# A hybrid decoder layer: one more shared pair, a combination that writes PSUM from VectorE, and other first and last transfers

## The chip, the core and the metric

The kernel runs on one core of a Trainium2 chip. The metric is the device time of one execution in microseconds (us). PE is TensorE (matmuls), DVE is VectorE, ACT is ScalarE, POOL is GpSimd, and SP is the engine that issues most transfers. PSUM is the memory that matmuls add up in; DVE and ACT can read and write it too.

## The reference

One decoder layer on 256 rows of width 2048, in float32. `SPLITS` cuts the projection into the gated recurrence's part (convolution, recurrent scan, gelu gate) and retention's part (rotary q and k, decayed scores, group norm, swish gate). The feed-forward width is 5632.

```
u = rmsnorm(h, ln1_w[l])
proj = jnp.einsum('bsd,de->bse', u, w_in[l])
lru_x, lru_g, q, k, v, ret_g = jnp.split(proj, SPLITS, axis=-1)
...
y = jnp.concatenate([y_lru, y_ret], axis=-1)
h = h + jnp.einsum('bse,ed->bsd', y, w_out[l])
u = rmsnorm(h, ln2_w[l])
ff = jax.nn.silu(jnp.einsum('bsd,df->bsf', u, w_ffn_gate[l])) * jnp.einsum('bsd,df->bsf', u, w_ffn_up[l])
h = h + jnp.einsum('bsf,fd->bsd', ff, w_ffn_down[l])
...
return rmsnorm(h, final_norm_w)
```

## The kernel before

**Split products.** Each operand is split in two float32r parts: ACT casts (`wh`, L122) and DVE subtracts (`wl`, L123). A product of two such operands is three matmuls, `wh` x `ah`, `wl` x `ah` and `wh` x `al`, in `three` (L682 to L684). One matmul has 128 stationary columns and 512 moving ones.

**Pairs.** From the out-projection on, a product is done by pairs of 128-row slices of the contraction: a 2 x 2 arrangement of left parts (a11 ... a22, the two halves of the 256 rows) and of weight parts (b11 ... b22, 512 columns each), into four PSUM accumulators c11, c12, c21, c22. A *plain* pair (letter `p` in `STEPS`, or two letters `h` for its halves) takes 8 products, 24 matmuls. A *shared* pair takes 7: its sums (t1 to t4 from the weights, L660; s1 to s4 from the left parts) go in four products that are made during the block before (`s`, function `share`, 12 matmuls) and three that are made in the pair's own block (`d`, `direct`, 9 matmuls, for which the second weight half is loaded and split again). For a shared pair DVE forms t1 to t4 in place (`add`). `SUMMED` lists the shared pairs of each block.

**Combination.** After the last `s` of a block, the four accumulators of `share` hold sums that are still to be combined: c11 stays, and c12, c22 and c21 are computed from all four (L806 to L812) and written back to PSUM, where the next block's own products are added on top. There are 13 such combinations, blocks 1 to 12 and the first of the two down blocks.

**Blocks and order.** Blocks 0 and 1 are the out-projection, 2 to 12 the gate/up projection (512 columns of w_gu each), then two blocks of the down projection. After a gate/up block, ACT's Silu and a DVE step (L878) give `gated`, which PE turns (`ft`, L867) into the left operand of the down projection. `make_left(i)` casts and splits such a left operand; the down block calls it before the weights of pair i. `program` is the list of steps; each step's loads are issued `AHEAD` = 3 ahead of it on SP's queue, and the Tile framework orders each engine's instructions by its own estimate of times. `hooks` names what is done at a given pair of the down blocks: `rows_back` brings residual rows back from DRAM by POOL's queue, and `load_fw` loads the final norm's weights there. Weights pass through 7 raw buffers and the pools of `split_tiles`; 60 buffers of 512 columns (`act_tile`) hold most of the rest.

**Start.** The first product is `v`: for each k of 16, x's slice of 128 columns is scaled to `u` (L297, L298) by ACT and DVE, from `small` (norm weights and biases, 104 columns), and PE runs 6 matmuls (L173 to L175). `load_x` issues the slices between the weight halves: `small`, slices 0 and 1 apart, then pairs. `squares` later sums the squares of x by ACT and POOL.

## Time and profile before

| | us |
|---|---|
| median of 3 runs | 1082.88 (1081.78 to 1082.94) |
| the profiled execution | 1082.31 |
| its span, first to last instruction | 1080.5 |
| PE busy | 1069.9 (99%) |
| DVE busy | 965.8 (89%) |
| ACT busy | 664.4 (61%) |
| POOL busy | 55.8 (5%) |
| mean granted TensorE clock | 0.998 |

The span leaves out 1.8 us around the program. "Busy" counts an engine's instructions; PE's matmuls overlap, so a row's duration is longer than the distance to the next one. A row such as `PE c L682 <- ACT sh L122: 0.3, 1, 0.3` says that PE, at line 682, waited for ACT's result of line 122: in all, how often, and the longest.

### The profile page before, as it was taken

The numbers are of one execution on the slowest core, as the hardware profiler recorded it, in microseconds if no ns is written. First come the engines' busy times: TensorE is split into PE (matmuls) and PEld (weight loads), VectorE is DVE, ScalarE is ACT, GpSimd is POOL, SyncE is SP. The second block draws the span as 40 slices with busy tenths as digits, with TensorE's granted clock in tenths as the row PEclk, the third lists the DMA queues.
The fourth block names the chain that finished last, engine by engine and source line by source line (L and its number), as shares of the span: only waits on it lengthen the run. The fifth ranks groups of instructions, "written<-read, shape, count | busy, mean of one in ns | idle before, by whom it ended". The sixth has DMA issues, their size and how long they took to land.

```text
span 1080.5 us, 14585 instructions
## 1 busy us (share of the span) xinstructions
PE 1069.9 (99%) x5086; PEld 896.5 (83%) x5086; DVE 965.8 (89%) x1400; ACT 664.4 (61%) x948; POOL 55.8 (5%) x73
## 2 busy tenths in 40 slices
PE   9999999999999999999999999999999999999997
PEld 7888888888888888888888888888888888888886
DVE  7789899988878889989999999999989899997994
ACT  7656744468746776656656565665656666555562
POOL 0602230000000000000000000000000000001001
PEclk9999999999999999999999999999999999999999
DMA  9964575554557588667777777787776846567562
GB/s 330 349 213 155 176 252 164 188 176 156 195 195 234 180 306 278 233 228 252 258 273 227 258 255 239 259 279 234 252 256 210 291 141 213 184 203 277 189 220 78
DMA packets 71387, 244.62 MB, mean 226 GB/s; under 512 B 8209, under 2 KB 8593, under 8 KB 71313
## 3 DMA queue, kind: packets, MB, share of 16 engines
q1 hardware_dynamic: 68400, 236.34, 64.2%
q0 software_dynamic: 1472, 4.72, 1.3%
q10 hardware_dynamic: 1440, 2.62, 0.6%
q8 instruction: 40, 0.66, 0.2%
q14 instruction: 35, 0.28, 0.1%
HBM read 239.46 MB, written 4.19 MB: 225 GB/s over the span
## 4 chain that ended last, share of the span: by engine, by line
PE 96%; POOL 1%; DVE 1%; DMA 1%; issue 0%; ACT 0%; SPq 0%; POOLq 0%; ACTq 0%
PE c L684 22%; PE c L683 22%; PE c L682 22%; PE fm L193 10%; PE fm L195 5%; PE tm L173 3%; PE tm L174 3%; PE tm L175 3%; POOL sumsq L309 1%; PE p L683 1%; PE p L682 1%; PE p L684 1%; PE ft L867 1%; DMA x<-in_x 1%; PE ht L587 0%
## 5 line engine op out<-in xcount | busy, mean ns | idle before, releaser
L122 ACT CAST wh<-raw 128x1024 fp32r<-128x1024 f32 (+1 forms) x499 | 463.0, 960 | 323.7 <-PE c L684 124.5
L123 DVE TENSOR_TENSOR wl<-raw,wh 128x1024 fp32r<-128x1024 f32 (+1 forms) x499 | 542.1, 1114 | 71.4 <-ACT wh L122 69.4
L683 PE MATMUL c<-wl,ah 128*128 128x512 f32 x820 | 320.0, 390 | 0.0
L684 PE MATMUL c<-wh,al 128*128 128x512 f32 x820 | 317.1, 389 | 0.0
L682 PE MATMUL c<-wh,ah 128*128 128x512 f32 x820 | 285.5, 391 | 0.0
L682 PEld LDWEIGHTS c<-wh,ah 128*128 128x128 f32 x820 | 153.9, 188 | 31.9 <-ACT wh L122 0.3
L684 PEld LDWEIGHTS c<-wh,al 128*128 128x128 f32 x820 | 153.9, 188 | 31.9 <-DVE al L123 0.3
L683 PEld LDWEIGHTS c<-wl,ah 128*128 128x128 f32 x820 | 154.0, 188 | 31.5
L193 PE MATMUL fm<-u,wh 128*128 128x512 f32 x512 | 161.3, 396 | 0.0
L195 PEld LDWEIGHTS fm<-u,wl 128*128 128x128 f32 x512 | 96.0, 188 | 22.5
L195 PE MATMUL fm<-u,wl 128*128 128x256 f32 x512 | 100.9, 278 | 0.0
L660 DVE TENSOR_TENSOR raw<-raw,raw 128x512 f32<-128x512 f32 x116 | 79.7, 687 | 2.2 <-DMA raw<-in_w_down 0.4
L660 DVE TENSOR_TENSOR raw<-raw 128x512 f32<-128x512 f32 x116 | 78.9, 685 | 1.1
L193 PEld LDWEIGHTS fm<-u,wh 128*128 128x128 f32 x512 | 78.3, 189 | 0.3
L683 PE MATMUL c<-wl,sh 128*128 128x512 f32 x193 | 74.8, 389 | 0.0
L684 PE MATMUL c<-wh,sl 128*128 128x512 f32 x193 | 73.6, 389 | 0.0
L682 PE MATMUL c<-wh,sh 128*128 128x512 f32 x193 | 68.3, 391 | 0.3 <-ACT sh L122 0.3
L174 PE MATMUL tm<-wl,u 128*128 128x512 f32 x128 | 48.6, 392 | 0.0
L175 PE MATMUL tm<-wh,u 128*128 128x512 f32 x128 | 48.5, 390 | 0.0
L173 PE MATMUL tm<-wh,u 128*128 128x512 f32 x128 | 46.6, 393 | 1.4 <-ACT u L297 1.4
L1118 POOL DMA_DIRECT2D htok<-kept_rows x8 | 4.3, 542 | 794.9 <-DVE wl L123 704.1
L682 PEld LDWEIGHTS c<-wh,sh 128*128 128x128 f32 x193 | 36.2, 188 | 8.2 <-ACT sh L122 0.7
(249 smaller groups left out, 1062.0 us busy)
## 6 DMA issues: line engine op xcount, KB each, us to landing
raw<-in_w_gu SPq DMA_DIRECT2D x216, 512.0 KB, 5.1
raw<-in_w_down SPq DMA_DIRECT2D x91, 512.0 KB, 4.6
raw<-in_w_out SPq DMA_DIRECT2D x34, 512.0 KB, 3.8
raw<-in_w_lx SPq DMA_DIRECT2D x16, 512.0 KB, 6.7
raw<-in_w_k SPq DMA_DIRECT2D x16, 512.0 KB, 3.7
raw<-in_w_q SPq DMA_DIRECT2D x16, 512.0 KB, 3.8
raw<-in_w_rg SPq DMA_DIRECT2D x16, 512.0 KB, 3.5
raw<-in_w_lg SPq DMA_DIRECT2D x16, 512.0 KB, 3.5
```

The costliest lines, as they stand in the source:

```text
L122: act.copy(out=dst_h, in_=src)
L123: v.tensor_tensor(out=dst_l, in0=src, in1=dst_h.bitcast(F32), op=ALU.subtract)
L173: pe.matmul(ps, ah, wh, start=first, stop=False)
L174: pe.matmul(ps, ah, wl, start=False, stop=False)
L175: pe.matmul(ps, al, wh, start=False, stop=last)
L193: pe.matmul(ps, wh, hl, start=n + i == 0, stop=False)
L195: pe.matmul(ps[:, :S], wl, hl[:, :S], start=False, stop=n + i == len(order) - 1)
L309: pool.tensor_tensor(out=sumsq, in0=sumsq, in1=sq, op=ALU.add)
L660: v.tensor_tensor(out=dst, in0=a, in1=b, op=ALU.add)
L682: pe.matmul(p, ah, bh, start=first, stop=False, skip_group_check=onto)
L683: pe.matmul(p, ah, bl, start=False, stop=False, skip_group_check=onto)
L684: pe.matmul(p, al, bh, start=False, stop=last, skip_group_check=onto)
```

## The change

1. The last gate/up block shares four pairs where it shared three: pair 0 is no longer plain. `STEPS` of block 11 becomes that of blocks 4 to 10, and block 12 takes block 11's old one. PE's program goes from 5027 to 5024 rows.
2. In the combination, c21 is also copied to SBUF (`p7`), c12 is written by DVE's subtraction straight to PSUM, c22 is rewritten in place by a `scalar_tensor_tensor`, and c21 is ACT's copy of q.
3. `make_left(1)` to `make_left(4)` become steps of their own inside block 12.
4. The first slice of x and `small` come as one transfer `lead` (128 x 360); slices 1 and 2, 3 and 4, ... come in pairs, slice 15 alone. One buffer of rows is taken from the act pool instead, so its load comes elsewhere on SP's queue.
5. In the second down block the final norm's weights are loaded at pair 9 instead of 11, and the rows come back at pair 12 instead of 7.

```diff
-SUMMED = ((), (4, 5), (2, 3), (1, 2, 3)) + ((0, 1, 2, 3),) * 8 + ((1, 2, 3),)
+SUMMED = ((), (4, 5), (2, 3), (1, 2, 3)) + ((0, 1, 2, 3),) * 9
...
-STEPS = ("pppspppspp", "ppspdpsdpp", "pdpsdpspspp", "pspsdpsdpsdp") + ("psdhsdhsdhsdhp",) * 7 + ("psdpsdpsddp", "psdpsdpsdpp")
+STEPS = ("pppspppspp", "ppspdpsdpp", "pdpsdpspspp", "pspsdpsdpsdp") + ("psdhsdhsdhsdhp",) * 8 + ("psdpsdpsddp",)
...
+ASIDE = {(12, 0): 1, (12, 2): 2, (12, 4): 3, (12, 6): 4}
...
-    xpool = early.enter_context(tc.tile_pool(name="resid", bufs=8))
+    xpool = early.enter_context(tc.tile_pool(name="resid", bufs=7))
+    lpool = early.enter_context(tc.tile_pool(name="lead", bufs=1))
...
+    lead = lpool.tile([P, S + N_SMALL], F32, tag="lead", name="lead")
+    last = lpool.tile([P, S], F32, tag="last", name="last")
+    small = lead[:, S:]
...
-        return xt[k // 2][:, (k % 2) * S : (k % 2) * S + S]
+        if k in (0, KT - 1):
+            return last if k else lead[:, :S]
+        return xt[(k - 1) // 2][:, (k - 1) % 2 * S : (k - 1) % 2 * S + S]
...
-        htok[cb, t] = res_tile("htok")
+        htok[cb, t] = (res_tile if n else act_tile)("htok")
...
-            p1, p, q = (act_tile(x) for x in ("p1", "p", "q"))
+            p1, p7, p, q = (act_tile(x) for x in ("p1", "p7", "p", "q"))
             act.copy(out=p1, in_=ps["c11"])
+            act.copy(out=p7, in_=ps["c21"])
             v.tensor_tensor(out=p, in0=ps["c12"], in1=p1, op=ALU.subtract)
-            v.tensor_tensor(out=q, in0=p, in1=ps["c22"], op=ALU.subtract)
-            act.copy(out=ps["c12"], in_=q)
-            v.tensor_tensor(out=ps["c22"], in0=q, in1=ps["c21"], op=ALU.subtract)
-            v.tensor_tensor(out=ps["c21"], in0=ps["c21"], in1=p, op=ALU.subtract)
+            v.tensor_tensor(out=ps["c12"], in0=p, in1=ps["c22"], op=ALU.subtract)
+            v.tensor_tensor(out=q, in0=p7, in1=p, op=ALU.subtract)
+            v.scalar_tensor_tensor(
+                out=ps["c22"], in0=ps["c22"], scalar=-1.0, in1=q, op0=ALU.mult, op1=ALU.subtract
+            )
+            act.copy(out=ps["c21"], in_=q)
...
+                if (self.index, k) in ASIDE:
+                    program.append(([], lambda i=ASIDE[self.index, k]: make_left(i)))
                 program.append(([quad], run))
...
         if k == 0:
-            nc.sync.dma_start(out=small, in_=A["small"])
-        if k < 2:
-            nc.sync.dma_start(out=xt[0][:, k * S : k * S + S], in_=A["x"][0][:, k * S : k * S + S])
-        elif k % 2 == 0:
+            nc.sync.dma_start(out=lead, in_=A["lead"])
+        elif k == KT - 1:
+            nc.sync.dma_start(out=last, in_=A["last"])
+        elif k % 2:
             nc.sync.dma_start(out=xt[k // 2], in_=A["x"][k // 2])
...
-        rows_back(1, act_tile)
-
-    hooks = {0: {6: stop_more, 9: swap_back}, 1: {7: sums_end, 11: load_fw}}
+
+    hooks = {0: {6: stop_more, 9: swap_back}, 1: {7: sums_end, 9: load_fw, 12: lambda: rows_back(1, act_tile)}}
```

The first rows of SP's queue, before (names are buffers; `raw` are weights, halves of 128 x 512):

```order
L140 DMA raw_4_125<-in_w_v 128x512
L1028 DMA small_90<-in_small 128x104
L1030 DMA x_0_82<-in_x 128x256
L140 DMA raw_4_125<-in_w_v 128x512
L1030 DMA x_0_82<-in_x 128x256
L140 DMA raw_9_143<-in_w_v 128x512
L1032 DMA x_1_83<-in_x 128x512
L140 DMA raw_9_143<-in_w_v 128x512
L140 DMA raw_14_159<-in_w_v 128x512
L1032 DMA x_2_84<-in_x 128x512
L140 DMA raw_14_159<-in_w_v 128x512
```

and after:

```order
L146 DMA raw_4_128<-in_w_v 128x512
L1043 DMA lead_85<-in_lead 128x360
L146 DMA raw_4_128<-in_w_v 128x512
L1047 DMA x_0_87<-in_x 128x512
L146 DMA raw_9_145<-in_w_v 128x512 x2
L1047 DMA x_1_88<-in_x 128x512
L146 DMA raw_14_161<-in_w_v 128x512 x2
L1047 DMA x_2_89<-in_x 128x512
L146 DMA raw_19_177<-in_w_v 128x512 x2
L1047 DMA x_3_90<-in_x 128x512
```

`small` and one transfer of x are gone, `lead` is wider, and x's pairs begin with slice 1, one place earlier than the pair of slices 2 and 3 stood.

DVE around the last combination, in block 12, before (c12_1668, c22_1666 and c21_1667 are the down block's accumulators; wl are splits of weights):

```order
L123 TENSOR_TENSOR wl_1729_8192<-raw_1727_8189,wh_1728_8191 128x1024
L123 TENSOR_TENSOR wl_1721_8152<-raw_1719_8149,wh_1720_8151 128x1024
L123 TENSOR_TENSOR wl_1726_8162<-raw_1722_8155,wh_1725_8161 128x1024
L808 TENSOR_TENSOR p_1714_8126<-c12_1668_7925,p1_1713_8125 128x512
L809 TENSOR_TENSOR q_1715_8127<-p_1714_8126,c22_1666_7917 128x512
L123 TENSOR_TENSOR wl_1734_8202<-raw_1730_8195,wh_1733_8201 128x1024
L811 TENSOR_TENSOR c22_1666_7917<-q_1715_8127,c21_1667_7921 128x512
L812 TENSOR_TENSOR c21_1667_7921<-c21_1667_7921,p_1714_8126 128x512
```

and after (c12_1693, c22_1691; L893 is the old L878, on block 12's own accumulators):

```order
L129 TENSOR_TENSOR wl_1749_8239<-raw_1747_8236,wh_1748_8238 128x1024
L129 TENSOR_TENSOR wl_1752_8245<-raw_1750_8242,wh_1751_8244 128x1024
L129 TENSOR_TENSOR wl_1746_8224<-raw_1744_8221,wh_1745_8223 128x1024
L819 TENSOR_TENSOR p_1739_8197<-c12_1693_8000,p1_1737_8195 128x512
L129 TENSOR_TENSOR wl_1760_8287<-raw_1758_8284,wh_1759_8286 128x1024
L129 TENSOR_TENSOR wl_1757_8281<-raw_1755_8278,wh_1756_8280 128x1024
L820 TENSOR_TENSOR c12_1693_8000<-p_1739_8197,c22_1691_7992 128x512
L821 TENSOR_TENSOR q_1740_8198<-p7_1738_8196,p_1739_8197 128x512
L129 TENSOR_TENSOR wl_1772_8344<-raw_1765_8328,wh_1771_8343 128x1024
L893 SCALAR_TENSOR_TENSOR gated_1753_8254<-c12_1601_7599,r2_tok_113,gated_1753_8254 128x512
L893 SCALAR_TENSOR_TENSOR gated_1754_8262<-c22_1599_7591,r2_tok_113,gated_1754_8262 128x512
L822 SCALAR_TENSOR_TENSOR c22_1691_7992<-c22_1691_7992,q_1740_8198 128x512
```

p and the writes of the accumulators now stand further apart; two splits stand between p and c12, and block 12's last two gated steps ahead of c22. The order of the three results was c12 (through q and ACT), c22, c21 and is c12, q for c21, c22.

PE at the end of block 12, before (c_1587 to c_1590 belong to block 12, c_1665 to c_1668 to the down block):

```order
L683 MATMUL c22_1588_7565<-wl_1721_8152,ah_847_4128 128x512
L684 MATMUL c22_1588_7565<-wh_1720_8151,al_848_4129 128x512
L682 MATMUL c11_1665_7913<-wh_1725_8161,ah_1723_8157 128x512
L683 MATMUL c11_1665_7913<-wl_1726_8162,ah_1723_8157 128x512
L682 MATMUL c12_1668_7925<-wh_1725_8161,ah_1723_8157 128x512
L683 MATMUL c12_1668_7925<-wl_1726_8162,ah_1723_8157 128x512
L682 MATMUL c22_1666_7917<-wh_1725_8161,ah_1723_8157 128x512
L683 MATMUL c22_1666_7917<-wl_1726_8162,ah_1723_8157 128x512
L682 MATMUL c21_1667_7921<-wh_1725_8161,ah_1723_8157 128x512
```

and after, where c12 begins (c_1690 is c11; its first row stands directly behind block 12's last, 15 matmuls ahead of c12's):

```order
L692 MATMUL c11_1690_7988<-wh_1756_8280,ah_1721_8121 128x512
L693 MATMUL c11_1690_7988<-wl_1757_8281,ah_1721_8121 128x512
L694 MATMUL c11_1690_7988<-wh_1756_8280,al_1722_8122 128x512
L692 MATMUL c11_1690_7988<-wh_1759_8286,ah_1658_7856 128x512
L693 MATMUL c11_1690_7988<-wl_1760_8287,ah_1658_7856 128x512
L694 MATMUL c11_1690_7988<-wh_1759_8286,al_1659_7857 128x512
L692 MATMUL c12_1693_8000<-wh_1745_8223,ah_1710_8078 128x512
L693 MATMUL c12_1693_8000<-wl_1746_8224,ah_1710_8078 128x512
```

Before, the four accumulators of the down block are all used within its first 7 matmuls; after, five pairs' products onto c11 come first, then those onto c12, c21 and c22.

More of the change, by code (lines that the diff above doesn't have):

```diff
@@ L93, in aux @@
         return paux.tile([P, 512], F32, tag="aux", name=nm(name))
+    lead = lpool.tile([P, S + N_SMALL], F32, tag="lead", name="lead")
+    last = lpool.tile([P, S], F32, tag="last", name="last")
+    small = lead[:, S:]
     xt = []
-    for i in range(KT // 2):
+    for i in range(KT // 2 - 1):
         xt.append(xpool.tile([P, 512], F32, tag="xh", name=f"x_{i}"))
-    small = cpool.tile([P, N_SMALL], F32, name="small")
     def xs(k):
-        return xt[k // 2][:, (k % 2) * S : (k % 2) * S + S]
+        if k in (0, KT - 1):
+            return last if k else lead[:, :S]
+        return xt[(k - 1) // 2][:, (k - 1) % 2 * S : (k - 1) % 2 * S + S]
     ident = cpool.tile([P, P], F32, name="ident")
@@ L306, in squares @@
             sq = act_tile("sq") if i else sumsq
-            act.activation(out=sq, in_=xt[i], func=AF.Square)
+            if i < KT // 2 - 1:
+                act.activation(out=sq, in_=xt[i], func=AF.Square)
+            else:
+                act.activation(out=sq[:, :S], in_=lead[:, :S], func=AF.Square)
+                act.activation(out=sq[:, S:], in_=last, func=AF.Square)
             if i:
@@ L1216, in cols @@
         return a.reshape(-1, P).T
+    x = g["x"][0].T.reshape(KT, P, S)
     arrays = {
-        "x": g["x"][0].T.reshape(KT // 2, 2, P, S).transpose(0, 2, 1, 3).reshape(KT // 2, P, 512),
-        "small": np.concatenate(
+        "x": x[1:-1].reshape(KT // 2 - 1, 2, P, S).transpose(0, 2, 1, 3).reshape(KT // 2 - 1, P, 512),
+        "last": x[-1],
+        "lead": np.concatenate(
             [
+                x[0],
                 cols(g["ln1_w"][0]), cols(g["ln2_w"][0]), cols(g["conv_w"][0].reshape(-1)), cols(g["conv_b"][0]),
```

## The prediction

> **What bounds the kernel now.** I read the first part of the page, then the waits of TensorE (PE), then windows over the stages that the change touches, then the timeline of the first 12 us.
>
> ```profile
> PE 1069.9 (99%) x5086; PEld 896.5 (83%) x5086; DVE 965.8 (89%) x1400; ACT 664.4 (61%) x948; POOL 55.8 (5%) x73
> ```
>
> Each entry is an engine's busy time and its share of the span. PE is never free for long; DVE is the next one. The waits of PE (who waited, for whom, us in total, times, the longest) name what it waited for by this profile; a row on the warm-up is left out:
>
> ```profile
> PE tm L173 <- ACT u L297: 1.4, 2, 0.9
> ...
> PE c L682 <- ACT sh L122: 0.3, 1, 0.3
> ```
>
> So a gain can come from fewer matmuls, or from the 1.4 us at the start. A loss comes from any engine that lets PE wait. Windows over two early full gate/up blocks, and then over the last two (from one block's transposes to the next's), show how near DVE is to that; columns are PE, PEld, DVE, ACT, POOL busy, the granted clock, DMA share and rate:
>
> ```profile
> 526.01:568.84 42.83, 42.83 (x195) 35.54 (x194) 40.72 (x52) 25.69 (x34) 0.00 (x0) 1.00 0.76 262
> 568.84:610.78 41.94, 41.94 (x191) 34.78 (x190) 39.98 (x52) 25.64 (x34) 0.00 (x0) 1.00 0.76 245
> ...
> 776.33:820.79 44.46, 44.46 (x202) 36.82 (x201) 40.05 (x53) 25.36 (x34) 0.00 (x0) 1.00 0.72 244
> 820.79:861.36 40.57, 40.57 (x184) 33.40 (x183) 37.07 (x51) 27.30 (x35) 0.00 (x0) 1.00 0.76 259
> ```
>
> In 526.01 to 610.78 DVE is busy 80.70 of 84.77 us (95%) and PE has no gap. In the last two blocks DVE has 77.12 of 85.03 us, so 7.9 us free.
>
> **Part 1: three matmuls fewer.** A plain pair costs 24 matmuls; a shared one costs 12 in the block before it and 9 in its own. PE has 5024 rows after, 5027 before. The spacing is read from PE's timeline at the end of block 12, of which these are the first and the last of 14 rows:
>
> ```profile
> 849.66 0.39 PE L683 MATMUL c<-wl,ah 128*128 128x512 f32 x1
> ...
> 852.61 0.39 PE L683 MATMUL c<-wl,ah 128*128 128x512 f32 x1
> ```
>
> (852.61 − 849.66)/13 = 0.227 us each (the 0.39 overlap). Three fewer give −0.68 us, all of it on the path, since PE has no gap there.
>
> The price is on DVE. The newly shared pair needs four sums (L660), three splits of 512 columns and two of 1024 where plain needs two of 1024. The rows give the shortest, median and longest in ns:
>
> ```profile
> L660 DVE TENSOR_TENSOR raw<-raw,raw x116: 678/686/695, 303.0 to 1037.9; 128x512 f32<-128x512 f32 x116
> ...
> L123 DVE TENSOR_TENSOR wl<-raw,wh x499: 673/1217/2318, 4.2 to 1049.6; 128x1024 fp32r<-128x1024 f32 x131, 128x512 fp32r<-128x512 f32 x36
> L123 DVE TENSOR_TENSOR t4l<-raw,t4h x45: 678/683/687, 306.8 to 841.6; 128x512 fp32r<-128x512 f32 x45
> ...
> L122 ACT CAST wh<-raw x499: 603/1051/1118, 3.5 to 1045.6; 128x1024 fp32r<-128x1024 f32 x131, 128x512 fp32r<-128x512 f32 x36
> L122 ACT CAST t4h<-raw x45: 611/617/626, 305.3 to 838.5; 128x512 fp32r<-128x512 f32 x45
> ```
>
> The split of the 1024-wide forms takes 1.22 us (the median; most of the 499 are that wide), the 512-wide 0.68. In block 11, which does the share: four sums 4 × 0.686 = 2.74, the splits of b11, t2 and t4 3 × 0.68 = 2.05, that of t1 and t3 together 1.22: +6.0 us. In block 12 the second half alone is loaded and split, 1.22 in place of 2.44: −1.2 us. So DVE gets 4.8 us more in a stretch with 7.9 us free, which leaves about 3.1 less the 0.68 that PE gives up, 2.4 of 84.4 us, or 97% busy. The row nearest to that is one block that ran at this share and cost PE nothing:
>
> ```profile
> 484.95:526.01 41.06, 41.06 (x188) 34.03 (x186) 39.72 (x52) 25.98 (x35) 0.00 (x0) 1.00 0.75 259
> ```
>
> 39.72 of 41.06 is 97%, over half the length. I take 0 for the wait of PE and keep as its other end that none of the free time can be used: 4.8 us of DVE work plus PE's own 0.68, or 5.5. ACT casts the same columns, block 11's more by 3 × 0.62 + 1.05 = 2.9 us; that and the 512 KB which block 12 reloads are costed at nothing: ACT is busy 25 to 27 us of a 41 to 44 us window, and the DMA share there is 0.72 to 0.76. Without that cover the 2.9 us would be PE's.
>
> **Part 2: the combination, 13 times.** Before: two copies on ACT, four operations on DVE. After: three copies, still four on DVE.
>
> ```profile
> L807 ACT COPY p<-c x13: 569/575/589, 328.6 to 839.0; 128x512 f32<-128x512 f32 x13
> ...
> L809 DVE TENSOR_TENSOR q<-p,c x13: 676/678/686, 332.1 to 848.1; 128x512 f32<-128x512 f32 x13
> ...
>   ACT c L810: 7.4, 5
> ...
> L811 DVE TENSOR_TENSOR c<-q,c x13: 684/686/689, 333.9 to 849.8; 128x512 f32<-128x512 f32 x13
> ...
> L878 DVE SCALAR_TENSOR_TENSOR gated<-c,r_tok,gated x22: 737/741/754, 433.4 to 856.3; 128x512 f32<-128x512 f32 x22
> ```
>
> c12 used to go p, q on DVE, copy on ACT, where ACT stood still for q in 5 cases, 7.4 us; now p and one DVE operation into PSUM. No row shows that operation with a PSUM result and a PSUM source; L811 is the same shape (0.686 us) and writes PSUM, so c12 is ready about one 0.58 us copy sooner. The new c22 has a scalar step; its nearest row is L878 (0.741), +0.055 us, 0.7 us in 13 combinations. ACT gets 13 × 0.575 = 7.5 us, spread over 500 us where it is 61% busy. Who waits: PE's next matmul onto c12, c22 and c21. In the last combination of before c21 was ready latest, and its DVE row shows the room:
>
> ```profile
> 847.37 0.69 DVE L808 TENSOR_TENSOR p<-c,p 128x512 f32<-128x512 f32 x1
> 848.09 0.69 DVE L809 TENSOR_TENSOR q<-p,c 128x512 f32<-128x512 f32 x1
> ...
> 850.43 0.69 DVE L812 TENSOR_TENSOR c<-c,p 128x512 f32<-128x512 f32 x1
> ```
>
> It ended at 851.12 and PE needed c21 when it came to the seventh matmul of the down block (851.02 + 6 × 0.227 = 852.4), 1.3 us later. In the new order c12 is first used 15 matmuls into that block, c21 30, c22 45 (make_left(1) to make_left(4) run ahead, so PE goes accumulator by accumulator). From the start of c12's last shared matmul to its next use are 24 matmuls, 5.45 us, less the 0.39 that this matmul lasts; in them DVE runs p, two splits and the new c12: 0.69 + 2.44 + 0.69 = 3.82. So 1.2 us of room where 1.3 was, and c21 follows 0.69 + 0.58 us later with 3.4 us of matmuls in between. Queued behind the copy p7 on ACT, which now also waits for c21's last matmul, are casts of weights that PE wants later. So 0 for this part and the ASIDE entries; below zero nothing, since PE's waits name no accumulator there, above it the 0.7 us of DVE, if all of that reached PE. The room of 1.2 us is DVE's lead; if it is gone, PE waits at this place for the same splits as in part 1.
>
> **Part 3: the first transfers.** The first fence has the issues on SP's queue (start, duration), the second the time to landing of those issued at 2.11, 2.59, 3.06 and 3.54, from the DMA view of each of these moments, the third rows of the timelines of ACT and PE:
>
> ```profile
> 2.11 0.43 SPq L140 DMA_DIRECT2D raw<-in_w_v  x1
> 2.59 0.43 SPq L1030 DMA_DIRECT2D x<-in_x  x1
> 3.06 0.43 SPq L140 DMA_DIRECT2D raw<-in_w_v  x1
> ```
>
> ```profile
> raw<-in_w_v SPq DMA_DIRECT2D x1, 256.0 KB, 3.7
> ...
> x<-in_x SPq DMA_DIRECT2D x1, 128.0 KB, 4.3
> ...
> raw<-in_w_v SPq DMA_DIRECT2D x1, 256.0 KB, 5.4
> ...
> x<-in_x SPq DMA_DIRECT2D x1, 256.0 KB, 5.5
> ```
>
> ```profile
> 6.93 0.51 ACT L297 ACTIVATE u<-x,small 128x256 fp32r<-128x256 f32 x1 [0.47 <-DMA x<-in_x]
> 8.44 0.62 ACT L122 CAST wh<-raw 128x512 fp32r<-128x512 f32 x1 [1.00 <-DMA raw<-in_w_v]
> ...
> 4.92 0.71 PE L173 MATMUL tm<-wh,u 128*128 128x512 f32 x2
> ...
> 7.49 0.73 PE L173 MATMUL tm<-wh,u 128*128 128x512 f32 x2 [0.93 <-ACT u L297]
> ...
> 9.66 0.73 PE L173 MATMUL tm<-wh,u 128*128 128x512 f32 x2 [0.52 <-ACT u L297]
> ```
>
> x1 (issued at 2.59, 4.3 to land) comes at 6.9; ACT makes u of it from 6.93 on, and the second k starts at 7.49, 0.58 after the landing. The third k waits for [x2 | x3] (3.54 + 5.5 = 9.1), and starts at 9.66. Each k is 6 × 0.227 = 1.36 us, so the third k's wait is the one that sets the end: a gapless run would have begun at 9.66 − 2.73 = 6.93, against 7.49 − 1.36 = 6.13 for the second. After, there is one issue fewer ahead; x1 and x2 come in one transfer, issued at about 2.11. Counting bytes, 948 KB are on their way by its end, between x1's 820 KB at 6.9 and the 1076 KB of the third weight half at 3.06 + 5.4 = 8.4 (KB added up in the order of issue: 256, 52, 128, 256, 128, 256): half way, 7.7. Then the second k starts at 7.7 + 0.58 = 8.25, as late as 8.25 − 1.36 = 6.89: the gain is 0.04. Counting from the issue instead, 2.11 + 4.3 = 6.4 at best and the second k at 7.0; then the third weight half, sooner by one issue (0.47 us) at 7.9, and its 0.62 us cast let the third k start at about 8.6: an early begin of 5.9, gain 1.0. If x1 comes only when that weight half came (8.4), the second k starts at 9.0, and 0.7 is lost. I take −0.3, nearer to the bytes since late landings in these rows grow with what was issued before them, with ends −1.0 and +0.7.
>
> The Trainium skill, "DMA: Bandwidth & Descriptors", section "Queues, rings and completion order", speaks against this part: descriptors of one queue are consumed in ring order on each DMA engine, so x1 cannot be announced before x2's bytes are through too. By it alone the gain is the 0.04 worked out from bytes; the times to landing that grow from 3.7 to 5.5 us down the queue agree.
>
> **Part 4: the later rows.** The four kept rows come back after the last norm's weights fw, and fw two quads earlier. Before, the later pair of fw was issued at 990 in quad 11:
>
> ```profile
> 989.97 1.06 POOL L895 DMA_DIRECT2D fw<-in_final_norm_w  x2 [3.92 <-PE c L684]
> ```
>
> ```profile
> htok<-kept_rows POOLq DMA_DIRECT2D x4, 256.0 KB, 7.5
> ```
>
> Behind the place of fw, at about 992 to 995 (one quad of weights later), they would land by some 1003. What uses them is the last block's sum of rows:
>
> ```profile
> 1038.52 0.68 DVE L923 TENSOR_TENSOR htok<-htok,part 128x512 f32<-128x512 f32 x1
> ```
>
> That is 35 us later: 0. The x_tok load moved on SP's queue stands between weight transfers that PE does not wait for.
>
> **The sum.** 1082.31 (the profiled execution; span 1080.5) − 0.68 − 0.3 + 0 = 1081.3. The median of the runs shown is 1082.88, 0.57 above it; I go half way, a base of 1082.6, so 1081.6.
>
> **Rivals.** (a) The start wins all of it: from the base 1082.6 − 0.68 − 1.0 = 1080.9, and down to 1079.9 if the third k too is freed of its wait (the first k began at 4.92, so at most 2.0 is there). For it: fewer and longer rows, one issue less. Against: one more 128 KB ahead of x1. Chance 0.20. (b) The start wins nothing or loses, by the ring order: 1081.9 to 1082.6. For it speak the growing times to landing. Chance 0.15. (c) DVE becomes the bound in blocks 11 and 12: slower. The page's groups say where DVE's free time lies (after the bar: busy, mean ns, idle before and most of its cause):
>
> ```profile
> L122 ACT CAST wh<-raw 128x1024 fp32r<-128x1024 f32 (+1 forms) x499 | 463.0, 960 | 323.7 <-PE c L684 124.5
> L123 DVE TENSOR_TENSOR wl<-raw,wh 128x1024 fp32r<-128x1024 f32 (+1 forms) x499 | 542.1, 1114 | 71.4 <-ACT wh L122 69.4
> ```
>
> It stands before splits that wait for ACT's casts, and these wait for PE to give buffers back, so the 7.9 us may not be usable; then up to 5.5 us go to PE, 1082.6 − 1.0 + 5.5 = 1087.1. It decides from 3.4 us on (1085.05, 0.2% over the median). Against it stand the blocks at 95 and 97% with no wait of PE. Whole: 0.09; a part of it, 1 to 2 us, 1082.6 to 1083.6: 0.14. (d) That a change does not do what it says: the direct write of c12 frees nothing, since no wait of PE is named there; this is in the forecast already.
>
> **Chances.** The forecast, 0.42, has its own range from 1081.0 to 1082.3. About 0.2% (2.2 us) is what a measurement of this kernel can tell from no change, so faster means below 1080.7: (a)'s better part and a low median, 0.20. Slower, above 1085.05: 0.09. Same: 0.71. The range goes from (a)'s end 1079.9 to 1083.9, past the partial (c), and leaves out 0.15 or so.
>
> **What would show it.** Right: PE's waits for u fall from 1.4 to about 1 us, the third k starts at 9.2 to 9.7; no wait of PE on c L693 or the like in blocks 11 and 12, DVE at 96 to 98% there. Wrong: a wait of PE for DVE's wl between 776 and 866, or at a first use of c12; a second k later than 8.6; a first use of c22 that waits behind the two gated steps.

## The result, and the profile after

The changed kernel takes 1089.57 us, the median of 4 runs (1089.46 to 1089.68), beside 1082.91 (1081.78 to 1083.62) of the kernel before on the same chip, 4 runs too. By means, with all runs of the kernel before on that chip, that is 1.0067 times as long, with a 95% interval from 1.0055 to 1.0078. The forecast was 1081.6 with a range up to 1083.9, so it was wrong in sign. The profiled execution took 1089.66 (span 1087.9, before 1080.5). The page's busy line:

```profile
PE 1074.0 (99%) x5083; PEld 897.0 (82%) x5083; DVE 971.4 (89%) x1407; ACT 672.9 (62%) x965; POOL 56.3 (5%) x73
```

The shares are the same as before: no engine has visibly become the bound. The waits of PE (who waited, for whom, us in total, times, longest) had two rows worth naming before, u 1.4 and sh 0.3. Now:

```profile
PE p L693 <- DVE wl L129: 1.6, 1, 1.6
...
PE p L692 <- ACT wh L128: 1.0, 1, 1.0
PE c L692 <- ACT c L825: 1.0, 1, 1.0
...
PE c L692 <- ACT ah L128: 0.2, 1, 0.2
PE c L693 <- DVE wl L129: 0.2, 1, 0.2
```

The wait for u isn't in the list any more; waits for a split, for a cast and for the combination's last copy (L825) have come. (`ah`, `sh` and `bh` are casts of left parts, of their sums and of weight halves, `al`, `sl` and `bl` the splits that go with them.) To see where the time went, I took from both timelines of PE when it reaches the same matmul, counted from the end of the program. Against before, PE is 0.85 us ahead when the first product is done; it loses 2.06 from the first combinations to the start of the first down block (the 0.68 of the three matmuls saved is in this sum), and 5.85 in the two down blocks; 0.3 more lies behind the last matmul: +7.4. Nearly all of it is lost at four places; 0.2 is spread over the blocks between the first two.

**At 521 us (+1.3).** The first combination writes c21 last, by ACT's copy of q. DVE's row of q, and ACT's rows around the copy:

```profile
519.20 0.68 DVE L821 TENSOR_TENSOR q<-p,p 128x512 f32<-128x512 f32 x1
```

```profile
519.49 1.26 ACT L891 ACTIVATE gated<-c,r_tok 128x512 f32<-128x512 f32 x2
520.65 1.56 ACT L128 CAST wh<-raw 128x1024 fp32r<-128x1024 f32 x2
522.10 0.59 ACT L825 COPY c<-q 128x512 f32<-128x512 f32 x1
```

q is ready at 519.88, and the copy of 0.59 us starts at 522.10, because two Silus and two casts stand ahead of it on ACT. PE waits 1.0 us for it.

**At 843 to 866 (+1.3)**, in block 12 and the beginning of the first down block, in losses of 0.2 to 0.4 us each, behind DVE as well as ACT:

```profile
843.63 0.50 PE L693 MATMUL c<-wl,ah 128*128 128x512 f32 x1 [0.21 <-DVE wl L129]
866.10 0.50 PE L692 MATMUL c<-wh,ah 128*128 128x512 f32 x1 [0.22 <-ACT ah L128]
```

**At 960 to 976 (+1.9).** The windows of the end of the first down block and of the second, before and then after (columns: length, then PE, PEld, DVE, ACT, POOL busy with counts, granted clock, DMA share, GB/s):

```profile
776.33:861.36 85.03, 85.03 (x384) 70.22 (x383) 77.12 (x103) 52.66 (x69) 0.00 (x0) 1.00 0.74 251
...
945.00:960.00 15.00, 15.00 (x68) 12.43 (x67) 13.74 (x18) 7.43 (x11) 0.00 (x0) 1.00 0.69 243
960.00:975.00 15.00, 15.00 (x67) 12.39 (x67) 13.70 (x17) 9.50 (x15) 2.12 (x4) 1.00 0.56 184
...
1005.00:1015.00 10.00, 10.00 (x46) 8.29 (x45) 10.00 (x13) 5.97 (x7) 0.00 (x0) 1.00 0.84 263
```

```profile
776.33:861.36 85.03, 84.73 (x379) 69.51 (x378) 80.81 (x110) 54.90 (x74) 0.00 (x0) 1.00 0.76 255
...
945.00:960.00 15.00, 15.00 (x68) 12.33 (x66) 10.56 (x12) 7.94 (x11) 0.00 (x0) 1.00 0.62 212
960.00:975.00 15.00, 14.45 (x62) 11.11 (x60) 14.31 (x20) 6.62 (x12) 1.07 (x2) 1.00 0.47 143
...
1005.00:1015.00 10.00, 8.27 (x29) 5.87 (x28) 10.00 (x12) 6.22 (x7) 0.00 (x0) 0.83 0.61 190
```

PE's loss, 1.4 of it between 974 and 976, begins some 20 us earlier, where PE is still full: DVE does 10.56 us of work where it did 13.74. DVE's rows with the idle time ahead of them, after and then before, and ACT's, after:

```profile
955.11 0.69 DVE L959 TENSOR_TENSOR htok<-c,htok 128x512 f32<-128x512 f32 x1 [3.42 <-PE c L694]
956.47 0.69 DVE L948 TENSOR_TENSOR n<-p,part 128x512 f32<-128x512 f32 x1 [0.67 <-PE p L694]
```

```profile
949.81 0.69 DVE L933 TENSOR_TENSOR n<-p,part 128x512 f32<-128x512 f32 x1 [1.04 <-PE p L684]
```

```profile
955.83 0.60 ACT L996 ACTIVATE c<-htok 128x512 f32<-128x512 f32 x1 [6.12 <-DVE htok L959]
956.96 2.96 ACT L128 CAST wh<-raw 128x1024 fp32r<-128x1024 f32 x3 [0.41 <-ACT c L996]
```

DVE's new order puts the block's first sum of rows (L959), which has to wait for PE's last matmul onto that accumulator, ahead of its other work; before, such sums stood behind splits, at 956.42, and waited for nothing. DVE stands 3.42 us. ACT stands 6.12 us for L996, which reads that sum and has casts behind it in its queue: weights that landed at 951.16 and 953.95 aren't cast before 956.96, and DVE's next split starts at 959.00. Splits free the raw buffers, so SP issues no transfer from 951.71 to 960.25 (before the gap was 948.80 to 953.59). The chain of what is late then goes transfer, cast, split, and PE meets it at 974: 1.0 us for wh.

**At 1007 to 1014 (+3.9).** DVE's rows there, then PE's, and the row of before for the same four products with fw:

```profile
1004.84 0.68 DVE L1001 TENSOR_TENSOR htok<-htok,fw 128x512 f32<-128x512 f32 x1
1005.44 0.69 DVE L670 TENSOR_TENSOR raw<-raw,raw 128x512 f32<-128x512 f32 x1
1006.05 0.68 DVE L1001 TENSOR_TENSOR htok<-htok,fw 128x512 f32<-128x512 f32 x1
1006.65 1.22 DVE L129 TENSOR_TENSOR wl<-raw,wh 128x1024 fp32r<-128x1024 f32 x1
1007.78 1.29 DVE L1001 TENSOR_TENSOR htok<-htok,fw 128x512 f32<-128x512 f32 x2
1008.99 4.62 DVE L129 TENSOR_TENSOR wl<-raw,wh 128x1024 fp32r<-128x1024 f32 x4
```

```profile
1010.26 0.80 PE L693 MATMUL p<-wl,sh 128*128 128x512 f32 x1 [1.58 <-DVE wl L129]
...
1013.77 0.39 PE L693 MATMUL c<-wl,ah 128*128 128x512 f32 x1
```

```profile
1013.35 2.49 DVE L986 TENSOR_TENSOR htok<-htok,fw 128x512 f32<-128x512 f32 x4
```

Before, the products stood together at 1013.35. With fw two pairs sooner they are ready to be ordered sooner, and stand among the splits that PE needs next, in a stretch in which DVE was already busy 10.00 of 10.00 us. By the starts of PE's matmuls (0.227 us apart when nothing is late) some 0.3 us are lost at 1007.7, 1.9 at the wait that the row gives as 1.58, and 1.7 up to 1013.77 by matmuls that start 0.43 us apart (1005 to 1015 has a mean clock of 0.83). How little slack there was is seen in the chain of the window 945 to 1020, whose by-line summary reads before:

```profile
by line: PE c L682 26.6%; PE c L683 26.6%; PE c L684 26.6%; PE p L683 7.0%; PE p L684 6.9%; PE p L682 6.7%
```

All of it is PE. After, the chain's summary for the same window begins with 18.3% in the transfers `raw<-in_w_down`, 12.9% in DVE's splits and 11.4% in its sums: the chain runs through DMA and DVE, so the weights that are late since 951 have a part in this wait too; no_hooks and no_mults below show how much.

### The profile page after: what moved, and what is told of

It reads as the page before. It is cut to its first block, busy times and chain, and to the rows that moved or that the text cites. A ratio compares the mean times of both kernels' runs of the same rounds, so it can differ in the third digit from the quotient of the medians.

```text
span 1087.9 us, 14615 instructions
## 1 busy us (share of the span) xinstructions
PE 1074.0 (99%) x5083; PEld 897.0 (82%) x5083; DVE 971.4 (89%) x1407; ACT 672.9 (62%) x965; POOL 56.3 (5%) x73
## 4 chain that ended last, share of the span: by engine, by line
PE 87%; DVE 6%; ACT 2%; DMA 2%; issue 2%; POOL 1%; POOLq 0%; ACTq 0%; DVEq 0%
PE c L693 19%; PE c L694 19%; PE c L692 19%; PE fm L199 10%; PE fm L201 5%; PE tm L179 3%; PE tm L180 3%; PE tm L181 3%; DVE wl L129 2%; DVE raw L670 2%; DMA raw<-in_w_down 1%; ACT wh L128 1%; POOL sumsq L319 1%; PE ft L882 1%; PE p L693 1%
## 5 line engine op out<-in xcount | busy, mean ns | idle before, releaser
L692 PE MATMUL c<-wh,ah 128*128 128x512 f32 x814 | 277.6, 392 | 1.3 <-ACT c L825 1.0
L694 PE MATMUL c<-wh,sl 128*128 128x512 f32 x197 | 76.1, 389 | 0.0
L694 PEld LDWEIGHTS c<-wh,sl 128*128 128x128 f32 x197 | 37.0, 188 | 7.7
```

Source lines behind the costliest of these rows:

```text
L692: pe.matmul(p, ah, bh, start=first, stop=False, skip_group_check=onto)
L694: pe.matmul(p, al, bh, start=False, stop=last, skip_group_check=onto)
```

## The experiments

Five parts can be put on or off: S, the share and the steps; A, the `ASIDE` entries; C, the combination; T, the first transfers; H, the later rows and the earlier fw (`hooks`). The changed kernel is all five. The table has each run's median (us), its ratio to the kernel before with the 95% interval, and three stages of its trace: how much later PE gets through the start, from there to the down blocks, and through the down blocks (us against before; the three matmuls saved are in the middle one where S is on).

| label | parts | median | ratio | start | middle | down |
|---|---|---|---|---|---|---|
| changed kernel | S A C T H | 1089.57 | 1.0067 [1.0055, 1.0078] | −0.85 | +2.06 | +5.85 |
| no_aside | S C T H | 1090.34 | 1.0074 [1.0059, 1.0089] | −0.21 | +4.45 | +4.24 |
| no_comb | S A T H | 1085.91 | 1.0033 [1.0018, 1.0047] | −0.45 | +0.03 | +5.58 |
| no_share | A C T H | 1084.28 | 1.0019 [1.0010, 1.0029] | −0.23 | +1.29 | +0.79 |
| no_hooks | S A C T | 1088.65 | 1.0057 [1.0042, 1.0072] | −0.28 | +2.21 | +3.82 |
| no_start | S A C H | 1092.32 | 1.0085 [1.0069, 1.0100] | +0.32 | +2.89 | +6.60 |
| no_comb_no_hooks | S A T | 1084.92 | 1.0019 [1.0010, 1.0029] | −0.13 | +0.04 | +0.64 |
| start_alone | T | 1082.77 | 1.0004 [0.9995, 1.0013] | −0.19 | −0.01 | +0.50 |
| start_aside | A T | 1083.23 | 1.0008 [0.9998, 1.0018] | −0.26 | −0.15 | +0.76 |
| start_comb | C T | 1084.24 | 1.0019 [1.0010, 1.0028] | −0.66 | +1.40 | +1.03 |
| start_hooks | T H | 1084.18 | 1.0017 [1.0008, 1.0027] | −0.89 | −0.01 | +2.31 |
| start_share | S T | 1089.44 | 1.0074 [1.0057, 1.0090] | −0.51 | +5.68 | +1.81 |
| start_comb_dve | C' T | 1087.63 | 1.0048 [1.0035, 1.0062] | −0.47 | +4.34 | +0.20 |
| start_no_mults | T | 1082.87 | 1.0003 [0.9994, 1.0012] | +0.03 | 0.00 | +0.94 |
| no_mults | S A C T H | 1087.91 | 1.0051 [1.0036, 1.0066] | −0.95 | +3.81 | +3.16 |
| mults_on_pool | S A C T H | 1091.65 | 1.0090 [1.0076, 1.0104] | −0.28 | +2.44 | +6.67 |

None is faster than the kernel before. The stages are read from one trace for each kernel, and the profiled run isn't always near the median: that of no_comb is 1.8 us above it, that of no_comb_no_hooks 1.9 below. C' is a variant of C. The edits follow against the changed kernel or, where the label begins with start, against start_alone; that of start_comb_dve is against start_comb. Line numbers shift with an edit: L825 of the changed kernel, the copy to c21, is L824 in no_aside and start_comb.

The early sum of rows at 951 stands in five of the traces: the changed kernel, no_hooks, no_start, no_mults and mults_on_pool. Each of them loses 1.9 to 2.0 us between 945 and 976, and none of the others loses more than 0.01 there. These five have share, `ASIDE` and combination together, and no other has.

**no_aside.** Theories: the `ASIDE` entries, which bring c12 forward, do the harm; or they are needed.

```diff
-ASIDE = {(12, 0): 1, (12, 2): 2, (12, 4): 3, (12, 6): 4}
-                if (self.index, k) in ASIDE:
-                    program.append(([], lambda i=ASIDE[self.index, k]: make_left(i)))
```

> The changed kernel without the four own Left steps in block 12; the extra shared pair stays. Theory A: DVE's order at the end of the first down block has the splits ahead of the add from c11, so no large wait at 973 or 1007: 1083 to 1085 us. Theory C (the work of the extra shared pair): 1088 to 1090.

Its median is 0.8 us above the changed kernel's (the intervals overlap), where 1083 to 1085 was expected of the first theory, which falls; the early sum at 951 is gone, but the loss comes at other places. PE's waits name what comes instead: ACT's cast `ah`, 1.3 us, and a split:

```profile
PE p L692 <- DVE wl L128: 1.9, 1, 1.9
PE c L691 <- ACT ah L127: 1.3, 1, 1.3
```

**no_comb.** The combination of before put back.

```diff
-            p1, p7, p, q = (act_tile(x) for x in ("p1", "p7", "p", "q"))
+            p1, p, q = (act_tile(x) for x in ("p1", "p", "q"))
...
-            v.tensor_tensor(out=ps["c12"], in0=p, in1=ps["c22"], op=ALU.subtract)
+            v.tensor_tensor(out=q, in0=p, in1=ps["c22"], op=ALU.subtract)
+            act.copy(out=ps["c12"], in_=q)
...
```

> The changed kernel with the old combination. Theory A: DVE's order there has the splits ahead of the add from c11, so 1082 to 1084 us, and no wait for c21's copy at 521 (that alone 1.1 us). If the combination costs only that wait: 1088.5.

The middle stage falls from +2.06 to +0.03, the median by 3.7 us: it lies between the two expectations. The wait for ACT's copy at 521 is gone, and so is the early sum of rows on DVE at 951. The wait at 1007 stays:

```profile
PE p L693 <- DVE wl L129: 2.0, 1, 2.0
```

**no_share.** `SUMMED` and `STEPS` of before put back.

```diff
-SUMMED = ((), (4, 5), (2, 3), (1, 2, 3)) + ((0, 1, 2, 3),) * 9
+SUMMED = ((), (4, 5), (2, 3), (1, 2, 3)) + ((0, 1, 2, 3),) * 8 + ((1, 2, 3),)
...
```

> The changed kernel with three shared pairs in block 12 as before (three matmuls more). Theory A: DVE's queue has the add from c11 behind the p6 subtraction and splits there, so the waits at 973 and 1007 are gone: 1083 to 1084.5 us (with the 1.1 us wait for c21 at 521 kept, the 1.6 us between 843 and 866 gone, start gain 0.9 kept). Theory C (DVE's 4.8 us of work more in blocks 11 and 12 is what PE pays): also near 1083, but then no_aside stays at 1089.

5.3 us of the 6.7 go, the largest share for one part. Both theories expected that. C, by its totals here and in no_aside, was the nearer one, but no_comb has the same work on DVE and loses 0.03 in the middle, so the work alone isn't what PE pays. The wait for L825 at 521 stays (1.0 us): it belongs to the combination, not to the share. And with the hooks in place PE loses nothing around 1007: the four products stand at 1002.28 to 1006.96 here.

**no_hooks.** The hooks of before put back.

```diff
-    hooks = {0: {6: stop_more, 9: swap_back}, 1: {7: sums_end, 9: load_fw, 12: lambda: rows_back(1, act_tile)}}
+    hooks = {0: {6: stop_more, 9: swap_back}, 1: {7: sums_end, 11: load_fw}}
```

(and `rows_back(1, act_tile)` inside `sums_end`.)

> The changed kernel, but final-norm weights at pair 11 and kept rows at pair 7 as before. Theory A (order: with the rest of the change DVE's queue has the add onto htok from c11, which PE finishes late at the end of the first down block, ahead of four weight splits; that stops the weight transfers for 8.5 us and PE pays at 973 and 1007): the order of DVE stays as in the changed kernel, so 1089.0 to 1090.0 us with the waits at about 973 and 1007. Theory B (transfers: moving the POOL transfers of fw and rows made the second down block late): 1084 to 1085, no wait near 1007.

The median is 0.9 us less than the changed kernel's, just under theory A's range; the intervals overlap. The waits at 1007 shrink to under 1 us each, 1.5 us lost in all, and they are for ACT's casts; that would be the part of the late weights. The late cast at 974 stays.

**start_alone, start_comb.** The start only, and the start with the combination.

> The kernel before with only the first transfers changed (lead; slices 1 and 2 in one transfer). From the changed kernel's trace the third k starts 1.05 us sooner and PE is 0.9 us ahead at 370: 1081.5 to 1082.1 us, 0.8 to 1.1 below the kernel before, waits for u 0 to 0.8 us. If the rule of ring order held alone: no gain, 1082.3 to 1082.9.

> The kernel before with the first transfers and the new combination. The theory on the combination: c21 now takes a second hop through ACT, whose queue has two Silu and two casts ahead of the copy in block 5's combination, so PE waits for c L825 about 1.0 us at 521: start_alone plus 1.0 to 1.2 us, that one wait and no other. Rival: the wait belongs to the extra shared pair's order and is absent here: equal to start_alone within 0.3.

The start by itself changes nothing that can be measured, as the rival had it: its 0.19 us is less than the 0.50 that is lost later, around 1007. With the combination 1.5 us are lost (1.0 to 1.2 were expected), 1.40 in the middle stage, and the row of PE's waits is the same as in the changed kernel:

```profile
PE c L691 <- ACT c L824: 1.0, 1, 1.0
```

So the second hop of c21 over ACT costs PE 1.0 us with no other part but the start in place.

**start_comb_dve.** If that hop is the cause, writing c21 by DVE and leaving a copy of it to ACT for q should give it back.

```diff
-            act.copy(out=p7, in_=ps["c21"])
...
-            v.tensor_tensor(out=q, in0=p7, in1=p, op=ALU.subtract)
+            v.tensor_tensor(out=ps["c21"], in0=ps["c21"], in1=p, op=ALU.subtract)
+            act.copy(out=q, in_=ps["c21"])
...
-            act.copy(out=ps["c21"], in_=q)
```

> As start_comb, but c21 is written by DVE in place and ACT copies it to q for c22, which PE needs last; ACT has two copies in place of three. Theory (second hop for c21): no wait near 521, equal to start_alone within 0.3. Rival (DVE's backlog of 5 us at p is the cause): the wait of about 1 us stays.

The wait at 521 is gone, as expected, and yet the kernel is 3.4 us slower than start_comb. In the last combination PE now waits 2.9 us for a left operand:

```profile
PE c L691 <- ACT ah L127: 2.9, 1, 2.9
```

The timeline of ACT there shows that this cast stands behind casts and the new copy:

```profile
849.86 2.94 ACT L127 CAST wh<-raw 128x1024 fp32r<-128x1024 f32 x3 [2.53 <-PE c L693]
852.71 0.57 ACT L820 COPY q<-c 128x512 f32<-128x512 f32 x1
853.19 1.14 ACT L127 CAST ah<-ff 128x512 fp32r<-128x512 f32 x2
```

The wh casts wait 2.53 us for buffers that PE gives back, and PE soon waits for the `ah` behind them. So neither expectation held: the wait at 521 was the second hop's, but the total was not start_alone's. Taking one hop away moved another.

**no_comb_no_hooks, start_hooks.** Two parts off; and the hooks with the start alone (edits as in no_comb and no_hooks).

> As no_comb, and fw at pair 11, rows at pair 7 as before; DVE then has the four products behind the pair's sums and one split. Theory D: no_comb less its wait of 2.0 us and half-rate stretch at 1004 to 1012, 1082.0 to 1083.5 us. Rival E: within 1 us of no_comb's 1085.9.

> The kernel before with the first transfers and the later rows (fw at pair 9, rows at pair 12). The four products now stand one pair sooner on DVE, in one piece between a shared pair's sums, without the extra shared pair. Theory D: PE waits there for 1 to 2.5 us: 1083.5 to 1085.3. If the hooks cost only together with the extra shared pair: start_alone, 1082.8 within 0.4.

With the share and the `ASIDE` entries the trace is nearly as good as start_alone's (+0.04 and +0.64): DVE's window 776.33 to 861.36 has 79.37 us of work, and what PE waits there, 0.5 us for L820 the longest, takes back what the three matmuls save. The median is 1.0 us under no_comb's, and so still in rival E's range, not in D's. The profiled executions lie further apart, 1083.02 here and 1087.75 for no_comb, whose medians are 1084.92 and 1085.91; so the hooks' 1.0 is read from the medians, whose intervals overlap, and the traces show only the place. By its median this kernel is 2.2 us slower than start_alone, and where that goes no trace shows. start_hooks came out as theory D expected, and the wait for a split at 1007 appears there without share and combination:

```profile
PE c L692 <- DVE wl L128: 1.3, 1, 1.3
```

**start_share.** The share without its `ASIDE` entries.

> The kernel before with the first transfers and the extra shared pair (three matmuls fewer, 4.8 us of DVE more). Theory: DVE's new work is paid by PE between 840 and 866 only (1.5 to 3 us, as no_aside shows 3.1), the second down block as in start_alone: 1083 to 1085 us. Rival (97% of DVE costs nothing, the forecast's own view): 1081.8 to 1082.3.

This is 4 us above the theory's range. Without steps of their own the casts of the left operands stand on ACT behind two wh casts,

```profile
850.40 1.99 ACT L127 CAST wh<-raw 128x1024 fp32r<-128x1024 f32 x2 [0.25 <-PE c L693]
852.30 1.14 ACT L127 CAST ah<-ff 128x512 fp32r<-128x512 f32 x2
```

and PE waits twice:

```profile
PE c L691 <- ACT ah L127: 2.4, 1, 2.4
PE c L691 <- ACT c L819: 1.4, 1, 1.4
```

Behind the second wait, from 855 to 857, PE was granted a clock of 0.52, which adds to the loss. The extra share costs 5.68 us in the middle without the `ASIDE` entries and 0.04 with them; by the medians, and with what follows in the down blocks, 6.7 and 2.2 against start_alone.

**no_start, start_aside.** Is the start, which moves loads on SP's queue, behind the losses 500 to 1000 us later? And do the `ASIDE` entries by themselves harm?

> The changed kernel with the first transfers as before; from the 550th matmul on every engine's order is that of the changed kernel. If the start's gain (0.2 to 0.9 us in the traces so far) reaches the end: 1089.9 to 1090.4. If the start's gain is lost again in the second down block, where PE waits for the weights anyway: 1089.2 to 1089.8.

> The kernel before with the first transfers and the four own Left steps. Theory: with accumulator after accumulator in the first down block the last combination gets room and nothing new waits; 1082 to 1083.2. If that order alone makes the second down block late (waits at 973 or 1007): over 1084.5.

No to both: without the start all the losses are there (+2.89 and +6.60), and the entries alone are within 0.5 us of start_alone. no_start's runs spread from 1089.58 to 1093.39, so that it is slower than the changed kernel by 2.75 us, outside both expectations, isn't put down to the start. From PE's 550th matmul on the order on every engine is that of the changed kernel, so these differences don't come from the order; what they come from isn't shown.

**no_mults, mults_on_pool, start_no_mults.** The four products of fw at 1004 to 1009, left out in no_mults and start_no_mults (only the first line of the diff; the outputs of columns 0 to 1023 then lack the factor) or given to POOL.

```diff
-                defer(17 + 2 * cb + t, lambda: v.tensor_tensor(out=h, in0=h, in1=fw[cb], op=ALU.mult))
+                defer(17 + 2 * cb + t, lambda: pool.tensor_tensor(out=h, in0=h, in1=fw[cb], op=ALU.mult))
```

> The changed kernel with the four products htok by fw of columns 0 to 1023 (L1001) left out; so the output lacks that factor in those columns. All other instructions of DVE keep their order up to this place. Theory D (these 2.4 us on DVE ahead of the splits make PE's wait at 1007 to 1010 and the half-rate stretch behind it): the wait there falls from 1.6 us to 0.3 at most, and 1085 to 1086.5 us. Rival E (the weights' loop through raw buffers, late since 951, makes it): 1088.5 to 1089.6.

> The changed kernel with four products htok by fw of the second down block (L1001) on POOL in place of DVE. Theory D: these four, 2.4 us, stand on DVE between the sums of a shared pair and the splits that PE waits for at 1007 to 1010 (they could be put there since fw is loaded two pairs earlier): the wait of 1.6 us and the half-rate stretch behind it go, 1085.5 to 1087. Rival: PE's wait there comes from the late weights alone (DVE lost its lead at 951): 1088.5 to 1089.6.

> The kernel before with the first transfers, and without the four products htok by fw of columns 0 to 1023 (L995), so the output lacks that factor there. If the start's gain is real and start_alone gives it back at 1007 (0.5 us in its trace) since DVE has no room there: 1081.3 to 1082.2, and no PE wait near 1007. If the start gains nothing in the runs: 1082.5 to 1083.

Left out, the down stage falls from +5.85 to +3.16 (1007 is left with losses of 0.6 and 0.4 behind ACT's casts). The median falls by 1.7, between the two theories and with intervals that overlap; the trace's middle stage is worse by 1.75, at 841 to 868, for a reason that isn't shown. On POOL they made it slower (the intervals just touch): the wait for wh at 976 stays, and a longer one for wh comes at 990:

```profile
PE p L692 <- ACT wh L128: 3.6, 2, 2.6
```

In start_no_mults, where they stood at 1013, nothing is gained by leaving them out, as in no_share, where they cost nothing. So they cost by their place, not by their length: of the 3.9 us at 1007 to 1014, 2.4 (no_hooks) to 2.7 (no_mults) are gone in these traces with the products away from there, and 1.2 to 1.5 stay, with the late weights.

## Why the prediction was wrong, point by point

**Part 1, the matmuls: right.** With the old combination and hooks (no_comb_no_hooks) the middle stage, which holds the −0.68, comes out at +0.04, start_alone at −0.01. So the three matmuls are gone, and waits of about 0.7 stand beside them.

**Part 1, "I take 0 for the wait of PE": mis-sized, and it depends on other parts.** DVE was forecast at 97% and is at 80.81 of 85.03, 95%, with 4.2 us free. In the changed kernel the place costs 1.3 us, and the first wait there is the one that the forecast named as a sign of being wrong, PE for DVE's wl (0.21 at 843.63); the last is for ACT's `ah`. Where the place costs most, the wait is ACT's: `ah` and c behind casts that wait for PE. The forecast had costed ACT's extra 2.9 us at nothing because ACT was busy 57 to 67%. With `ASIDE` and the old combination that nearly held (0.04 and 0.03 in two traces, the matmuls saved included); with the share alone it was 5.68 us. That is near the 5.5 us of rival (c), by another engine.

**Part 2, "0 for this part": wrong.** PE waits 1.0 us at 521 in every kernel with the new combination, and loses 1.5 from the first combinations to 780, by the step that said "queued behind the copy p7 on ACT ... are casts". It looked at what stands behind ACT's copies, not at what stands ahead of the last of them: c21 was written by DVE directly and now needs a second hop, which waits 2.2 us in ACT's queue. The room that was worked out, 1.2 us of DVE's lead, held no such queue, and it was that of the last of 13 combinations, while the wait came at an earlier one. Next to the share the part cost 3.7 us by the medians (no_comb against the changed kernel). By the traces 2.0 of that are in the middle stage; the 1.9 of the early sum of rows at 951, which comes only with share, `ASIDE` and combination together, is the rest by its size, but no_comb's trace loses 1.7 more than the changed kernel's around 1007, so the sum doesn't close.

**The `ASIDE` entries, 0: right alone, and they help.** +0.5 us alone, which the intervals do not tell from none; with share and start they take off 4.5 (start_share against no_comb_no_hooks).

**Part 3, "I take −0.3": near in size, which its own end doesn't explain.** PE's rows at the beginning of the first, second and third k:

```profile
4.96 1.22 PE L179 MATMUL tm<-wh,u 128*128 128x512 f32 x2
...
7.25 0.61 PE L179 MATMUL tm<-wh,u 128*128 128x512 f32 x2
...
8.61 0.63 PE L179 MATMUL tm<-wh,u 128*128 128x512 f32 x2
```

The third k starts at 8.61, 1.05 us before the 9.66 of before; the forecast had 9.2 to 9.7. In this trace the end "counting from the issue", which gave 8.6 for it, came out: the transfer of slices 1 and 2 landed at 6.20, where the issue gave 6.4 and the bytes 7.7. That PE doesn't wait for u here is in part PE's own doing: its first five matmuls start 0.38 to 0.59 us apart, so the first k takes 2.28 us where six of 0.227 take 1.36. But this trace is an exception. Over the 15 traces with the new start that transfer landed between 5.94 and 7.57, with a median of 7.30, nearer to the bytes; the third k's median start is 9.38, in the forecast's range, and 13 of them keep a wait for u of 0.2 to 1.6 us. Of the 1.05 us 0.85 are left when the first product is done; over the 15 traces that gain has a median of 0.28, from 0.95 down to a loss of 0.03. The two traces with the old start (before and no_start) differ by 0.31 themselves, so a gain of 0.3 can't be told from none, and that the forecast hit the median is luck in part. It doesn't reach the time: start_alone is within 0.2%.

**Part 4, "35 us later: 0": wrong.** It asked when the rows and fw land and who needs them last, and not where the order of DVE puts the four products that fw releases. By the traces' down stage the hooks cost 2.0 us in the changed kernel (5.85 against no_hooks' 3.82) and 1.8 next to the start alone (2.31 against 0.50); by the medians 0.9, within the noise, and 1.4. In no_share they cost nothing around 1007.

**Rival (c)** gave 1087.1 and had the chance 0.09. Its total is nearest to the measured 1089.6, its place and engine are not: DVE at 776 to 861 has 4.2 us free, and the larger part was lost 110 to 150 us later.

The common fault: each part was costed alone, with a busy share over 40 us as its cover, and behind three of the four places the order of one queue, at 521, 951 and 1007, puts work that waits or could wait in front of what PE needs next. Against a sum of three zeros and −0.98 the trace has +1.5 for the combination up to 780, +1.3 at 843 to 866, +1.9 at 960 to 976 and +3.9 at 1007 to 1014. What stays open is why the parts add up as they do: next to the start alone the entries, the hooks and the combination cost 0.5 to 1.5 each, the share without its entries 6.7, and all five 6.7 against before, and why the scheduler moves the sum of rows with three parts and not with two.

## What to carry to other kernels

In this kernel a busy share of 60 or 95% covered nothing for an instruction whose queue holds one that waits for someone else: when an edit adds a hop on an engine, list what stands ahead of it there, at the place where PE will use it. Where a scheduler orders the program, read the order of the changed kernel at the tight stretches too (here those with DVE busy 10.00 of 10.00 us), even when the edit lies hundreds of microseconds away, and look for instructions that an earlier load releases. Test parts in pairs: here a part that cost 1.5 us with the start alone cost 3.7 beside the others, and one that looked needless saved 4.5.

## What the runs showed of the hardware

**Two short waits slowed PE more than a long one.** The clock column in windows of 2 us of the changed kernel, and of 4 us of start_comb_dve around its 2.9 us wait:

```profile
1008.00:1010.00 2.00, 0.68 (x3) 0.20 (x2) 2.00 (x3) 1.55 (x2) 0.00 (x0) 1.00 0.44 102
1010.00:1012.00 2.00, 1.74 (x4) 1.45 (x5) 2.00 (x3) 0.26 (x1) 0.00 (x0) 0.56 0.66 207
```

```profile
850.00:854.00 4.00, 1.10 (x6) 0.60 (x5) 3.88 (x5) 4.00 (x6) 0.00 (x0) 1.00 0.72 287
854.00:858.00 4.00, 3.36 (x13) 2.25 (x14) 4.00 (x7) 1.49 (x3) 0.00 (x0) 1.00 0.87 259
```

Between 1007 and 1010 PE stood for some 0.3 and 1.9 us and was granted 0.56 afterwards, which cost 1.7 more. At 850 it stood for 2.9, then for 0.6 at 855, and kept 1.00. no_start and start_hooks, whose longest wait of PE in the second down block is 1.3 us in both, differ in the same way: 0.50 from 1014 to 1016 in no_start, 1.00 from 1006 to 1010 in start_hooks. The Trainium skill, "TensorE: Matmul & The Clock Gate", section "Part 1: The HAM clock gate", has a free-running window of about 3.4 us, and the clock halved after an idle one. No wait in these rows lasted so long, so the clock fell here on less than a whole idle window; that a wait's place in the window matters more than its length would fit them, but these few cases don't prove it.

**DVE is slower beside POOL.** In mults_on_pool POOL's four products and DVE's rows in and after them:

```profile
980.64 7.22 POOL L1001 TENSOR_TENSOR htok<-htok,fw 128x512 f32<-128x512 f32 x4
```

```profile
983.24 1.78 DVE L129 TENSOR_TENSOR bl<-raw,bh 128x512 fp32r<-128x512 f32 x1
984.95 1.77 DVE L670 TENSOR_TENSOR raw<-raw,raw 128x512 f32<-128x512 f32 x1
...
988.93 0.68 DVE L670 TENSOR_TENSOR raw<-raw,raw 128x512 f32<-128x512 f32 x1
```

The same sum took 1.77 us beside POOL and 0.68 after it, and DVE's rows from 978 to 989 take some 4.4 us longer than their like elsewhere, so moving the products (2.5 us) off DVE took more of its time than it gave. The Trainium skill, "SBUF — State Buffer", section "SBUF: two separate sides", states that the two engines share a port pair under an exclusive lock, for DVE instructions with two SBUF inputs; the trace agrees, in that each DVE row takes about as long as one of POOL's (7.22/4 = 1.8 us).
